# A two-block transformer kernel whose instruction order is drawn up against another model of the machine

## The chip, the cores and the metric

The kernel runs on one core of one Trainium2 chip. The metric is device time in microseconds (us), lower is better; the time of a kernel is the median of its runs. Apart from those runs one execution was recorded by the hardware profiler, and every row in this document is from such a recording.

## The reference, cut to what matters

One sequence of 512 tokens, model width 1024, float32, goes through two blocks. The first block is a block-sparse attention beside a multi-scale pooling, then a squared-ReLU MLP. The second has an RWKV-7 mixer (a recurrence over the tokens), a three-branch sparse attention (NSA), a gated merge of the two, cross-attention to 256 memory tokens, and a convolutional feed-forward net.

```python
def first_block(x, ...):
    proj = rms_norm(x, norm_mix) @ w_in
    q, k, v, u = split(proj)
    a = moba_attention(q, k, v)                 # 8 heads, ALiBi
    p = multiscale_pool(u, w_pool, pool_scale)
    x = x + concat([a, p]) @ w_out
    h = rms_norm(x, norm_mlp)
    x = x + square(relu(h @ w_up)) @ w_down     # 1024 -> 4096 -> 1024
    return rms_norm(x, norm_final)

def second_block(x, mem, ...):
    z = rms_norm(x, norm_mix_2) @ w_in_2
    y_r = rwkv7_mixer(z_r, ...)                 # state = state*w + sa*b + v*k, token by token
    y_n = nsa_mixer(z_q, z_kc, ..., gates)      # 16 heads, 4 kv groups
    gm = sigmoid(z_m)
    merged = gm[0] * (y_r @ w_branch_rwkv) + gm[1] * (y_n @ w_branch_nsa)
    h = x + merged @ w_mix_out
    h = h + cross_attn(rms_norm(h), rms_norm(mem), ...)     # 4 heads
    return h + conv_ffn(rms_norm(h), ffn_up, ffn_conv, ffn_down)   # width 2816
```

## The kernel before

**Products.** Activations lie transposed, 128 features by 512 tokens to a tile. Every large product runs in three passes: both factors are split into a high part in the PE's fast 32-bit format and the remainder, and high x high, high x low and low x high are added up in PSUM. `gemm_g` does this: for each tile of 128 outputs and each group of eight 128-row slices, SP loads a 128x1024 weight tile `ws` (L209), ACT casts it to `wh` (L222), DVE subtracts to get `wl` (L223), and PE runs 24 matmuls of 512 columns (L243 to L245). `ws`, `wh` and `wl` have two buffers each; then `evac`, a function of the caller, takes the result out of PSUM. `gemm_tok_g` (L271 to L273) is the same with the roles of weights and activations exchanged. Products that belong to different streams are told apart by the tag of their PSUM bank: `psg`, `psg_p`, `psg_m`, `psg_b`.

**Stages.** By the trace's time: the first block's projections and attention (about 0 to 200 us), its MLP (to 580), the projections of the second block together with the preparation of the RWKV recurrence (to about 1050), the recurrence, the sparse attention and the merge (to about 1460), and the tail of output product, cross-attention and feed-forward net (to the end). Within a stage generators in Python are interleaved by `weave`: each generator yields an estimate of the PE time of what it has just emitted, and the one that is furthest behind its rate goes on. What comes out is one long program; the two stages in which three kinds of work are mixed are emitted by these two lines:

```python
g.weave(("", g.rwkv_fronts(xs), 245), ("_p", others(), 170))
...
g.weave(("", until("", g.nsa()), 190), ("_b", right(), 240), ("_m", until("_m", g.merge_gates(xs, range(49, 59))), 65))
```

`rwkv_fronts` makes decay, keys and values per pair of heads; in it `head_stats` squares the keys, adds them up on PE (L561), takes the reciprocal root by ten or so small DVE operations (L149 to L155), spreads it with one ACT copy (L570) and turns it back with four PE transposes (L573). `rwkv_solve` inverts small triangular matrices by 31 pairs of DVE operations (L777, L778), each of which needs the pair before. `rwkv_chain` is the recurrence: for each of 8 head pairs and 8 chunks it goes PE (L874), DVE (L875), PE (L888), DVE (L889), PE (L891), DVE (L897), each step needing the one before; `rwkv_finish` ends a head pair with transposes (L919). `nsa_groups` and `attend` are the attention (L311 to L333). `merge_gates` is a plain product, ten tiles of 24 matmuls in the second of the two stages (`psg_m`), and serves to fill PE.

**Order.** The engines run side by side, each through one list of instructions in a fixed order, and wait for each other by semaphores. The lists are not the order in which the Python code emitted the instructions. When the `TileContext` at L1602 closes, the framework plays the program on a model of the machine: whenever an engine is free in the model, it gets the instruction that is ready there and that stands earliest in the program; buffers of a pool are handed out in the same play. The order in which the model started the instructions becomes the list of each engine. The SP and POOL queues, which issue the DMAs, are ordered in the same way. An instruction that the model thought ready early, and that is late on the chip, holds up all that stands behind it on its engine.

## Time and profile before

| | |
|---|---|
| time of the kernel, median of 3 runs | 2091.92 us (2091.23 to 2095.46) |
| the profiled execution | 2094.42 us, its span 2092.6 us |
| busy in that span | PE 2015.6 us, PE weight loads 1635.5, DVE 1308.9, ACT 926.1, POOL 95.4 |
| mean granted clock of the PE | 0.975 |
| HBM | 205.12 MB read, 45.53 MB written, 120 GB/s over the span |

The span runs from the first to the last instruction; the 1.8 us between it and the execution's time lie outside. Busy time of the PE counts matmuls from issue to modelled end, and they overlap, so that a busy PE may still be a PE that does not run at full rate. The granted clock is a mean over the stretch, as a share of full speed (2.4 GHz); the clock has two levels here, 1.2 and 2.4 GHz.

### The profile page before, as it was taken

How to read it: one execution, taken by the hardware profiler on the slowest of the kernel's cores; microseconds unless marked ns; L12 is line 12 of the kernel's file. 1: busy time of each engine (PE TensorE's matmuls, PEld its weight loads, DVE VectorE, ACT ScalarE, POOL GpSimd, SP SyncE). 2: the span in 40 equal slices, each digit the busy share in tenths (PEclk: the TensorE clock that was granted, in tenths of full speed). 3: DMA queues.
4: the chain of work that ended last, by engine and by line, in shares of the span. 5: the costliest groups of instructions: out<-in, count | busy, mean ns of one | idle time of the engine just before them, and what ended most of it. 6: DMA issues, size and time to landing. Idle time of an engine off the chain costs nothing. (4 is left out here: it accounts for less than half of the span.)

```text
span 2092.6 us, 27828 instructions
## 1 busy us (share of the span) xinstructions
PE 2015.6 (96%) x9927; PEld 1635.5 (78%) x9927; DVE 1308.9 (63%) x3007; ACT 926.1 (44%) x1778; POOL 95.4 (5%) x167
## 2 busy tenths in 40 slices
PE   8999999999999999899989899999999999999999
PEld 7778888888887778777767688877878878888887
DVE  5785432554464569777668788878466756666522
ACT  5864531442253233233357477767143443333311
POOL 0000000000003201000120111000000000000000
PEclk9999999999999999999989799999999999999999
DMA  4223333333365655555574454445542123323332
GB/s 161 80 89 95 94 92 100 107 115 117 125 199 159 165 158 164 154 149 175 161 178 109 116 131 129 110 131 160 158 145 81 51 80 91 97 95 92 100 108 83
DMA packets 178266, 256.75 MB, mean 123 GB/s; under 512 B 95408, under 2 KB 109952, under 8 KB 178128
## 3 DMA queue, kind: packets, MB, share of 16 engines
q1 hardware_dynamic: 162832, 231.31, 38.1%
q0 software_dynamic: 15296, 23.66, 4.0%
q8 instruction: 79, 1.29, 0.3%
q14 instruction: 59, 0.48, 0.1%
HBM read 205.12 MB, written 45.53 MB: 120 GB/s over the span
## 5 line engine op out<-in xcount | busy, mean ns | idle before, releaser
L222 ACT CAST wh<-ws 128x1024 fp32r<-128x1024 f32 (+2 forms) x283 | 291.7, 1031 | 699.6 <-PE psg L244 459.4
L223 DVE TENSOR_TENSOR wl<-ws,wh 128x1024 fp32r<-128x1024 f32 (+2 forms) x283 | 339.5, 1201 | 263.5 <-ACT wh L222 262.3
L243 PE MATMUL psg<-xh,wh 128*128 128x512 f32 x984 | 392.1, 399 | 2.9 <-ACT wh L222 2.9
L245 PE MATMUL psg<-xh,wl 128*128 128x512 f32 x984 | 393.6, 400 | 0.0
L244 PE MATMUL psg<-act,wh 128*128 128x512 f32 x912 | 359.7, 395 | 1.1 <-DVE act L166 1.1
L243 PEld LDWEIGHTS psg<-xh,wh 128*128 128x128 f32 x984 | 185.9, 189 | 45.0 <-ACT wh L222 3.7
L245 PEld LDWEIGHTS psg<-xh,wl 128*128 128x128 f32 x984 | 186.1, 189 | 41.6 <-issue 1.2
L244 PEld LDWEIGHTS psg<-act,wh 128*128 128x128 f32 x912 | 171.1, 188 | 42.8 <-DVE act L166 1.5
L243 PE MATMUL psg<-act,wh 128*128 128x512 f32 x496 | 196.2, 397 | 2.8 <-ACT act L165 1.4
L245 PE MATMUL psg<-act,wl 128*128 128x512 f32 x496 | 196.0, 396 | 0.5 <-DVE wl L223 0.5
L244 PE MATMUL psg<-xl,wh 128*128 128x512 f32 x352 | 139.7, 397 | 0.0
L243 PEld LDWEIGHTS psg<-act,wh 128*128 128x128 f32 x496 | 92.8, 187 | 27.3 <-ACT act L165 2.2
L245 PEld LDWEIGHTS psg<-act,wl 128*128 128x128 f32 x496 | 93.0, 187 | 23.8 <-DVE wl L223 1.3
L315 ACT ACTIVATE p<-p,sm 128x128 f32<-128x128 f32 (+3 forms) x160 | 89.6, 561 | 18.8 <-DVE sm L313 17.7
L244 PE MATMUL psg<-x,wh 128*128 128x512 f32 x216 | 88.7, 411 | 0.0
L331 DVE TENSOR_TENSOR pt<-psb,pt 128x512 fp32r<-128x512 f32 (+3 forms) x160 | 75.6, 487 | 18.7 <-ACT pt L330 16.6
L313 DVE CUSTOM_DVE_ANT_0 p<-psa,bias 128x128 f32<-128x128 f32 (+3 forms) x160 | 76.0, 484 | 11.9 <-PE psa L312 9.7
L328 PE MATMUL psb<-ident,p 128*128 128x128 f32 x400 | 79.1, 292 | 2.2 <-DVE p L323 1.2
L330 ACT CAST pt<-psb 128x512 fp32r<-128x512 f32 (+3 forms) x160 | 65.9, 424 | 32.0 <-PE psb L328 29.4
L244 PEld LDWEIGHTS psg<-xl,wh 128*128 128x128 f32 x352 | 66.3, 188 | 14.1
L243 PE MATMUL psg_p<-xh,wh 128*128 128x512 f32 x176 | 72.8, 414 | 0.8 <-ACT f L957 0.6
L244 PE MATMUL psg_p<-x,wh 128*128 128x512 f32 x176 | 72.3, 411 | 0.0
(491 smaller groups left out, 3916.4 us busy)
## 6 DMA issues: line engine op xcount, KB each, us to landing
ws<-in_w_in SPq DMA_DIRECT2D x49, 512.0 KB, 4.0
ws<-in_w_fup SPq DMA_DIRECT2D x44, 512.0 KB, 3.5
ws<-in_w_up SPq DMA_DIRECT2D x32, 512.0 KB, 3.5
ws<-in_w_down SPq DMA_DIRECT2D x32, 512.0 KB, 3.6
ws<-in_w_fdn SPq DMA_DIRECT2D x16, 512.0 KB, 3.6
ws<-in_w_qku SPq DMA_DIRECT2D x12, 512.0 KB, 3.6
ws<-in_w_in POOLq DMA_DIRECT2D x10, 512.0 KB, 4.8
ws<-in_w_out SPq DMA_DIRECT2D x8, 512.0 KB, 3.5
```

Of the source, the lines that this page charges most:

```text
L222: nc.scalar.copy(wh[:, :n], ws[:, :n])
L223: nc.vector.tensor_tensor(wl[:, :n], ws[:, :n], wh[:, :n].bitcast(F32), OP.subtract)
L243: nc.tensor.matmul(p[:, :n], wh[:, s], h[:, :n], start=c + k == 0, stop=False)
L244: nc.tensor.matmul(p[:, :n], wh[:, s], l[:, :n], start=False, stop=False)
L245: nc.tensor.matmul(p[:, :n], wl[:, s], h[:, :n], start=False, stop=last)
L313: nc.vector.tensor_tensor_reduce(pt, ps[:, :w], bias[:, 512 - w:], 1.0, 3e38, OP.add, OP.min, m[:, i:i + 1])
L315: nc.scalar.activation(pt, pt, AF.Exp, bias=m[:, i:i + 1], scale=-1.0, accum_out=s[:, i:i + 1])
L328: nc.tensor.transpose(ps[:, (i - j) * 128:(i - j + 1) * 128], P[i][:, j * 128:j * 128 + 128], self.ident)
L330: nc.scalar.copy(ph[:, :w], ps[:, :w])
L331: nc.vector.tensor_tensor(pl[:, :w], ps[:, :w], ph[:, :w].bitcast(F32), OP.subtract)
```

## The change

One argument is added where the kernel opens the framework's context. The lists of all engines are then drawn up by playing the program on the framework's timeline model instead of on its default one. The rule by which an instruction is picked, the program that is played, every instruction and its operands' shapes, the pools and their numbers of buffers are the same; what can differ is the order on each engine, DMA queues included, which of a pool's buffers a tile gets, and with these the semaphore waits.

```diff
@@ -1599,7 +1599,7 @@
     nc = bacc.Bacc("TRN2", target_bir_lowering=False, num_devices=1)
     A = {k: nc.dram_tensor("in_" + k, v.shape, F32, kind="ExternalInput").ap() for k, v in arrays.items()}
     out = nc.dram_tensor("out_0", (D, T), F32, kind="ExternalOutput").ap()
-    with tile.TileContext(nc) as tc:
+    with tile.TileContext(nc, schedule_with_timeline_sim=True) as tc:
         emit(tc, A, out)
     r = run_bass_kernel_spmd(nc, [{"in_" + k: v for k, v in arrays.items()}], core_ids=[0])
     return np.ascontiguousarray(r.results[0]["out_0"].T)[None]
```

## Rows read from the trace of the kernel before

**Rows 1.** The page: span, and busy time of each engine.

```profile
span 2092.6 us, 27828 instructions
PE 2015.6 (96%) x9927; PEld 1635.5 (78%) x9927; DVE 1308.9 (63%) x3007; ACT 926.1 (44%) x1778; POOL 95.4 (5%) x167
```

**Rows 2.** Busy time by stage: stretch, its length, busy us of each engine, clock, DMA.

```profile
0.00:40.00 40.00, 33.89 (x232) 31.44 (x233) 23.19 (x48) 21.58 (x34) 0.20 (x4) 1.00 0.52 177
40.00:580.00 540.00, 537.50 (x2511) 435.44 (x2509) 285.80 (x516) 242.23 (x407) 0.95 (x1) 1.00 0.33 102
580.00:760.00 180.00, 172.81 (x906) 140.79 (x906) 99.92 (x197) 69.68 (x111) 30.61 (x51) 0.98 0.63 173
760.00:1060.00 300.00, 278.63 (x1419) 225.09 (x1418) 225.25 (x621) 104.17 (x158) 30.49 (x59) 0.96 0.58 163
1060.00:1440.00 380.00, 349.74 (x1999) 287.81 (x1998) 304.32 (x1035) 257.42 (x727) 33.12 (x52) 0.90 0.50 131
1440.00:1720.00 280.00, 274.63 (x1274) 217.47 (x1273) 178.26 (x348) 117.15 (x209) 0.00 (x0) 1.00 0.34 106
1720.00:2080.00 360.00, 359.90 (x1560) 290.93 (x1559) 191.10 (x244) 113.84 (x136) 0.00 (x0) 1.00 0.32 98
2080.00:2092.60 12.60, 8.52 (x37) 6.53 (x35) 1.05 (x2) 0.00 (x0) 0.00 (x0) 1.00 0.05 21
```

**Rows 3.** Waits of PE: total us, times, longest.

```profile
PE psn L573 <- ACT cx L570: 7.6, 1, 7.6
...
PE psn L919 <- ACT y L915: 5.4, 3, 3.0
PE psb_b L874 <- ACT vs L842: 4.9, 1, 4.9
PE psg L243 <- ACT wh L222: 3.7, 3, 2.9
PE psn L561 <- DVE vc L1098: 3.4, 1, 3.4
```

**Rows 4.** PE in order of time around the longest wait: start, duration, instruction.

```profile
870.07 0.40 PE L243 MATMUL psg_p<-xh,wh 128*128 128x512 f32 x1
878.07 1.12 PE L573 MATMUL psn<-ident,cx 128*128 128x128 f32 x4 [7.60 <-ACT cx L570]
878.83 0.78 PE L244 MATMUL psg_p<-x,wh 128*128 128x512 f32 x1
879.41 0.63 PE L245 MATMUL psg_p<-xh,wl 128*128 128x512 f32 x1
...
883.24 0.39 PE L243 MATMUL psg<-xh,wh 128*128 128x512 f32 x1
883.47 0.39 PE L244 MATMUL psg<-x,wh 128*128 128x512 f32 x1
```

**Rows 5.** DVE in order of time over the same stretch.

```profile
869.97 0.16 DVE L566 TENSOR_SCALAR sm<-psn 128x8 f32<-128x8 f32 x1
...
870.98 1.22 DVE L223 TENSOR_TENSOR wl<-ws,wh 128x1024 fp32r<-128x1024 f32 x1
...
876.96 0.16 DVE L155 SCALAR_TENSOR_TENSOR col<-sm,col 128x8 f32<-128x8 f32 x1
```

**Rows 6.** The recurrence's first matmul, by line: x count, ns min/median/max, first and last start.

```profile
L874 PE MATMUL psb_b<-vs,ws x128: 270/275/553, 1068.5 to 1417.3; 128*128 128x128 f32 x128
```

**Rows 7.** Groups by line, 1060 to 1440: count, busy us, mean ns, idle before.

```profile
L897 DVE SCALAR_TENSOR_TENSOR vs<-vs,decay,psb_b 64x64 f32<-64x64 f32 x96 | 26.7, 279 | 8.0 <-PE psb_b L891 5.8
...
L223 DVE TENSOR_TENSOR wl<-ws,wh 128x1024 fp32r<-128x1024 f32 x10 | 12.2, 1220 | 0.1
```

**Rows 8.** The matmuls of `psg_m` alone, three stretches of 20 us; clock next.

```profile
1160.00:1180.00 20.00, 0.00 (x0) 0.00 (x0) 0.00 (x0) 0.87 0.51 146
1180.00:1200.00 20.00, 0.46 (x2) 0.38 (x2) 0.00 (x0) 0.53 0.39 102
1200.00:1220.00 20.00, 7.91 (x27) 4.58 (x26) 0.58 (x1) 1.00 0.46 123
```

## The prediction

> **What bounds the kernel now.** I read the page first, for the share of each engine, then busy time by stage, then the waits of PE, the longest of them in order of time, and last the stage in which the recurrence runs. In the page the reader sees PE busy for all but 77.0 us of its 2092.6 us span and no other engine near that [rows 1]. By stage this falls apart into two kernels [rows 2]. From 40 to 580 us and from 1720 to 2080 us PE is without a gap to speak of (2.5 and 0.1 us idle) at full clock: in the latter 1560 matmuls take 360 us, one every 0.231 us, and an order of instructions can win nothing there, since the same matmuls have to pass. The first 40 us (6.1 us idle) wait for the first inputs, and the last 12.6 us (4.1 us) for the last result to leave. What is left between 580 and 1440 us is 860 us in which three kinds of work are mixed: idle 7.2, 21.4 and 30.3 us, 58.9 together, and a granted clock of 0.98, 0.96 and 0.90, which is 3.6, 12.0 and 38.0 us of full-speed time that PE was not given, 53.6 together. From 1440 to 1720 us another 5.4 us are idle. So this is where a change of order is won or lost: some 860 us out of 2093, with 58.9 us of gaps.
>
> **What such a gap is.** The longest one shows the kind. PE waits 7.6 us in one piece for a copy by ACT [rows 3]. In order of time [rows 4]: at 870.07 us PE runs a matmul of a large product (`psg_p`), then its list has the four transposes of `head_stats` (L573), whose input is late, and they start at 878.07 us. The next in the list is the second pass of that same product, over the weights `wh` of which the first pass had just run: it was ready all the time and stood behind. After the gap the matmuls come 0.58 us apart first, and 0.23 us apart again at 883 us. DVE was what made the input late: the reciprocal root begins at 869.97 us (L566) and its last small operation starts at 876.96 us, because between its links DVE's list has steps of the triangular solve and splits of weights, one of 1.22 us [rows 5]. Both lists were drawn up by a play in which the root was done sooner than it was. This is what another model of the machine can change, and it is the only thing.
>
> **The change part by part.** It removes and adds no instruction and no byte: 9927 matmuls, 3007 DVE and 1778 ACT instructions stay [rows 1], so the sum of work is 0 us on either side, and it is hidden by nothing because it does not change. What moves are places in the lists.
>
> (1) The unmixed stages, 900 us with their two long stretches: 0 us, bounded by their idle time, 2.6 us, on the side of a gain. On the side of a loss the cover is that a weight tile is loaded and split while the eight slices before it run, 24 matmuls of 0.231 us or 5.5 us, against 1.2 us on DVE for a split and about as much on ACT. Only an order that puts several long DVE operations ahead of a split uncovers it; DVE is busy 191 of 360 us there [rows 2], so I take 0.
>
> (2) The gaps of the mixed stages. Nothing in this trace shows the new order, so its worth is bounded by rows: below by nothing (each gap is only traded for another), above by all 58.9 us. Between these I take the five single waits of 2.9 us or more [rows 3]: 7.6 (L573), 4.9 (L874), 3.4 (L561), 3.0 (the longest of the three at L919) and 2.9 (L243), together 21.8 us. A model that has DVE's and ACT's small operations about right will not put a matmul before an input that is 3 us or more away while others are ready; that is the error of the present lists which the rows show. The other 37.1 us are gaps of under 2 us, smaller than the differences between any two orders, and I let them stand as moved.
>
> (3) The clock. Its 53.6 us are bounded the same way, between 0 and all. I take 0: the low clock is deepest where PE's work is thin, and part of it lies under the gaps counted already.
>
> (4) DMA queues and buffers. SP and POOL get a new order too. SP issues a weight load when a buffer comes free; the loads stand under the cover of (1). I take 0 here, and leave a loss to the rivals.
>
> The sum: span 2092.6 - 21.8 = 2070.8 us; with the 1.8 us outside the span 2072.6 us against the profiled execution's 2094.4; and as the median of the runs stands 2.5 us below the profiled execution, 2070 us.
>
> A rule of the Trainium skill speaks for less. "Perfetto Trace Analysis", section "Identifying the Most-Contended Engine", says that matmul busy time is not a good measure of how near PE is to its limit, and that the busy share of weight loads is one. By it the ceiling is lower: weight loads are busy 290.93 of 360 us (80.8%) where PE is full and 653.69 of 860 us (76.0%) in the mixed stages, so that these could shrink to 809 us, by 51 us instead of 112.5 for gaps and clock; the same share of that (21.8 of 58.9) would be 19 us and the time 2073 us. I keep the rows of single waits, which name their places.
>
> **The rivals.**
>
> *The recurrence is served later (slower).* From 1068.5 to 1417.3 us L874 runs for 64 steps [rows 6], two matmuls each: 348.8 us over 63 intervals, 5.54 us a step, in which DVE must be reached three times, for operations of about 0.28 us [rows 7]. DVE is busy 304.3 of 380 us there, with 1035 instructions, 0.294 us on average [rows 2]. If the new lists hand DVE and PE more of the attention's and the product's work as soon as it is ready, each visit of the recurrence finds one more instruction ahead: 3 x 0.294 x 63 = 56 us if the recurrence alone sets the stage. The attention runs beside it to the stage's end, so I count half, 28 us: 2120 us. It decides the sign once a step gets 0.35 us longer (21.8 / 63). For it: DVE has little slack there, and one split in front costs 1.22 us [rows 7]. Against it: the recurrence keeps its place in the program, and the rule of picking is the same.
>
> *The filler is spent early (slower).* The stage's plain product (`psg_m`) fills PE. Where it has none or two matmuls, the granted clock is 0.87 and 0.53; in the next 20 us, with 27, it is 1.00 [rows 8]. A play that finds PE free more often runs this product as soon as its weights are there, and leaves the end of the stage thin. If 100 us more run at 0.70 in place of 0.90, that is 20 us, and 2112 us. The low level is 1.2 of 2.4 GHz, so a matmul there takes twice as long. The Trainium skill points the same way: "Perfetto Trace Analysis", section "Matmul Optimizations", says that PE scales its power with its use and that matmuls should come back to back in batches; the rows just named agree, with 0.53 and 1.00.
>
> *No change.* The new lists differ, but gaps are traded one for one; or the option leaves the lists as they are. 2092 us. For it: two thirds of the time is indifferent to order. Against it: 860 us of three-way mixing rarely come out the same to 4 us.
>
> *More than the five.* All gaps of the mixed stages go: 2092 - 59 = 2033 us. For it: DVE would still have room (629.5 of 860 us busy). Against it: 30.3 of the 58.9 us lie where chains of small steps feed each other.
>
> **How the numbers follow.** The forecast (5 to 35 us faster) gets 0.38, more than that 0.11, no change 0.13, the recurrence served later 0.22, the filler spent early 0.16. What a measurement of this kernel can tell from no change is 0.2%, 4 us. So faster 0.49, same 0.13, slower 0.38. The likeliest case gives 2070 us, with a range of its own of 2057 to 2087. Over all cases I take 2034 (all gaps gone) to 2124 (the first rival and 4 us more); below lie about 0.04, above about 0.12.
>
> **What would show it.** Right: from 580 to 1440 us the same work takes about 840 us, with some 37 us idle, and among PE's waits no single one over 3 us between 600 and 1440 us; L573 is no longer ahead of a product's matmuls for microseconds; the stretches before 580 and after 1440 us are as long as before, to 3 us. The recurrence served later shows as more than 5.9 us from one step of L874 to the next. The filler spent early shows as an end of `psg_m` well before 1400 us and a clock under 0.85 behind it. It would make the prediction wrong if the unmixed stages got gaps: then weight loads or splits are late, and (1) was the step that failed; or if the gaps stayed and others came, then the present model's error was not what made them.

## The result and the profile after

The kernel got slower: 2223.05 us median (2218.63 to 2223.74, 4 runs) against 2093.69 us (2091.23 to 2096.67, 4 runs, one more than ahead of the prediction), a ratio of 1.0625 with a 95% interval of 1.0602 to 1.0648. The forecast was 2070 us, in a range that ended at 2124 us. Both the number and the sign were wrong.

The page of the changed kernel, span and busy time of each engine:

```profile
span 2221.8 us, 27961 instructions
PE 2057.5 (93%) x9927; PEld 1677.9 (76%) x9927; DVE 1322.8 (60%) x3007; ACT 927.5 (42%) x1778; POOL 99.7 (4%) x167
```

The reader sees the same counts as in [rows 1], so no work was added. The span grew by 129.2 us, of which 87.3 us are idle time of PE (164.3 in place of 77.0) and 41.9 us are busy time of the same 9927 matmuls. Most of this is the clock, whose mean over the span fell from 0.975 to 0.952: at its low level (1.2 GHz) PE was busy for 172.6 us in place of 94.9. Matmuls of one shape, first at the low and then at the full level:

```profile
804.41 0.63 PE L243 MATMUL psg<-xh,wh 128*128 128x512 f32 x1
804.84 0.63 PE L244 MATMUL psg<-x,wh 128*128 128x512 f32 x1
...
806.40 0.40 PE L243 MATMUL psg<-xh,wh 128*128 128x512 f32 x1
806.63 0.39 PE L244 MATMUL psg<-x,wh 128*128 128x512 f32 x1
```

They start 0.43 us and 0.23 us apart, so a matmul does not take twice as long at the low level, as the prediction had it, but somewhat less. By these numbers the low level accounts for some 36 of the 41.9 us (an estimate, 77.7 x (1 - 0.23/0.43)).

To see where, both kernels are cut at the same work and not at the same times: at the first L504 (end of the MLP), the first L833 (start of the recurrence stage), the last L333 (end of the sparse attention) and the last L1376 (end of the cross-attention). The busy time by stretch of the kernel before, cut so; columns as in [rows 2]:

```profile
0.00:567.70 567.70, 559.39 (x2648) 455.97 (x2649) 300.51 (x538) 257.03 (x432) 0.20 (x4) 1.00 0.34 106
567.70:1051.90 484.20, 457.35 (x2383) 372.04 (x2382) 328.52 (x837) 176.78 (x271) 57.96 (x104) 0.97 0.59 165
1051.90:1459.40 407.50, 375.23 (x2138) 307.75 (x2136) 326.58 (x1092) 278.89 (x778) 37.22 (x59) 0.91 0.50 131
1459.40:1681.60 222.20, 217.55 (x1014) 173.10 (x1013) 138.63 (x268) 83.07 (x142) 0.00 (x0) 1.00 0.35 107
1681.60:2092.60 411.00, 406.11 (x1752) 326.64 (x1750) 214.65 (x273) 130.31 (x158) 0.00 (x0) 1.00 0.31 95
```

And of the changed kernel:

```profile
0.00:584.80 584.80, 566.43 (x2670) 464.82 (x2671) 301.08 (x539) 257.19 (x432) 0.20 (x4) 0.99 0.33 104
584.80:1088.70 503.90, 461.41 (x2361) 375.80 (x2359) 335.54 (x835) 176.13 (x268) 58.34 (x98) 0.94 0.57 157
1088.70:1592.80 504.10, 431.85 (x2276) 359.95 (x2276) 346.26 (x1107) 287.53 (x787) 41.16 (x65) 0.86 0.44 118
1592.80:1808.60 215.80, 191.45 (x875) 151.00 (x874) 125.42 (x254) 76.50 (x134) 0.00 (x0) 0.98 0.28 86
1808.60:2221.80 413.20, 406.33 (x1752) 326.38 (x1750) 214.54 (x273) 130.18 (x158) 0.00 (x0) 1.00 0.31 95
```

The five differences are +17.1, +19.7, +96.6, -6.4 and +2.2 us. The fourth hides a loss: 139 fewer matmuls fall into it (they ran ahead, into the third), and in it the cross-attention itself, from its first L1356 to its last L1376, went from 68.2 to 85.4 us. So every stretch in which a chain of dependent steps runs beside a plain product lost, and the last one, plain products alone, hardly did.

The waits of PE in the changed kernel, as in [rows 3]:

```profile
PE psg L243 <- ACT wh L222: 11.7, 7, 8.3
PE psn_p L573 <- ACT cx L570: 9.8, 2, 9.2
PE psa L311 <- DVE sm L313: 8.9, 16, 1.7
PE psb_b L888 <- DVE rh L875: 7.8, 19, 0.7
...
PE psg_m L243 <- ACT f L957: 6.4, 2, 5.2
```

The wait on which the forecast rested, at L573, is still there and has grown from 7.6 to 9.2 us. The recurrence, as in [rows 6]:

```profile
L874 PE MATMUL psb_b<-vs,ws x128: 270/275/552, 1116.2 to 1515.8; 128*128 128x128 f32 x128
```

That is 399.6 us over 63 steps, 6.34 us a step in place of 5.54. But the 50.8 us are not spread over the steps: the first eight take 94.6 us in place of 49.2, and the other 55 take 5.54 us each in place of 5.44. Of the third stretch's 96.6 us some 11 lie ahead of the first L874 and some 35 behind the last, where the attention takes 76.9 us to its end in place of 42.1. And the filler, as in [rows 8]; the number before the last two of each row is the clock:

```profile
1180.00:1200.00 20.00, 11.88 (x44) 7.36 (x43) 1.19 (x2) 1.00 0.47 141
1200.00:1220.00 20.00, 3.42 (x14) 2.16 (x12) 0.60 (x1) 0.74 0.64 204
1220.00:1240.00 20.00, 0.00 (x0) 0.00 (x0) 0.00 (x0) 1.00 0.63 163
```

Its last matmul starts at 1203.4 us, ahead of the seventh of 64 steps of the recurrence; before, it lasted to 1425.0 us, past the last step. From 1240 to 1540 us the clock of the 20 us stretches is between 0.60 and 0.91.

Last, what happens to a step of the recurrence while the filler runs. DVE in order of time:

```profile
1197.64 0.30 DVE L889 COPY_PREDICATED vu<-blk,psb_b 128x128 f32<-128x128 int32 x1
1202.73 0.57 DVE L897 SCALAR_TENSOR_TENSOR vs<-vs,decay,psb_b 64x64 f32<-64x64 f32 x2 [4.79 <-PE psb_b L891]
```

PE over the same stretch:

```profile
1197.78 0.50 PE L245 MATMUL psg_m<-xh,wl 128*128 128x512 f32 x1
1198.11 0.39 PE L243 MATMUL psg_m<-xh,wh 128*128 128x512 f32 x1
...
1202.07 0.40 PE L245 MATMUL psg_m<-xh,wl 128*128 128x512 f32 x1
1202.31 0.38 PE L891 MATMUL psb_b<-vu,wl 128*128 128x128 f32 x2
```

DVE has finished L889 at 1197.94 us. The matmul that needs it, L891, starts at 1202.31 us: 18 matmuls of the filler stand between, run without a gap, and DVE is idle for 4.79 us. Since PE has no gap here, no view of PE's waits shows it.

One such place proves little: the kernel before has one of 5.03 us from L889 to L891, with 29 others between. What changed is the mean while the filler runs. Over the first eight steps, from L875 to L888 it is 3.4 us with 13.8 other matmuls between (before: 1.4 us, 6.0), and from L889 to L891 2.3 us with 9.8 (before: 0.9 us, 4.6). Over the later steps the two are nearly as before, 0.46 and 0.90 us in place of 0.48 and 0.80. In the attention it lasts through the stage: from the end of ACT's copy (L330) to the start of the matmul that uses it (L332), each copy taken with its own matmul, 128 times from the first L874 on, the mean is 0.39 us with 1.6 other matmuls between in the kernel before, and 2.01 us with 9.3 in the changed one. (The expectations below give 8.0 for the latter, which counts only to the next L332, also that of another copy.) Ready work waits for its turn, not for its input.

### The profile page after: what moved, and what is told of

It reads as the page before. It is cut to its first block, busy times and chain, and to the rows that moved or that the text cites. A ratio compares the mean times of both kernels' runs of the same rounds, so it can differ in the third digit from the quotient of the medians.

```text
span 2221.8 us, 27961 instructions
## 1 busy us (share of the span) xinstructions
PE 2057.5 (93%) x9927; PEld 1677.9 (76%) x9927; DVE 1322.8 (60%) x3007; ACT 927.5 (42%) x1778; POOL 99.7 (4%) x167
## 4 chain that ended last, share of the span: by engine, by line
PE 37%; DVE 6%; DMA 3%; ACT 3%; issue 2%; SPq 0%; POOL 0%; DVEq 0%; ACTq 0%
PE psg L243 7%; PE psg L244 7%; PE psg L245 7%; PE psg_b L245 1%; PE psg_b L243 1%; PE psg_b L244 1%; PE psb L328 1%; DMA ld<-vd 1%; PE pso L332 1%; PE pso L333 1%; PE psb_b L888 1%; DVE wl L223 1%; ACT p L315 1%; DVE pt L331 1%; DMA yc<-ydr 1%
## 5 line engine op out<-in xcount | busy, mean ns | idle before, releaser
L243 PE MATMUL psg<-xh,wh 128*128 128x512 f32 x984 | 393.5, 400 | 18.7 <-ACT wh L222 10.4
L243 PEld LDWEIGHTS psg<-xh,wh 128*128 128x128 f32 x984 | 186.7, 190 | 64.1 <-ACT wh L222 11.2
L243 PE MATMUL psg<-act,wh 128*128 128x512 f32 x496 | 197.0, 400 | 8.0 <-ACT act L162 3.4
L243 PEld LDWEIGHTS psg<-act,wh 128*128 128x128 f32 x496 | 92.8, 188 | 33.9 <-ACT act L162 4.6
L330 ACT CAST pt<-psb 128x512 fp32r<-128x512 f32 (+3 forms) x160 | 65.0, 423 | 45.4 <-PE psb L328 41.8
L243 PE MATMUL psg_p<-xh,wh 128*128 128x512 f32 x176 | 74.9, 425 | 4.3 <-DVE f L1035 2.6
L245 PE MATMUL psg_p<-xh,wl 128*128 128x512 f32 x176 | 73.4, 417 | 0.0
```

What stands on the lines that cost most here:

```text
L243: nc.tensor.matmul(p[:, :n], wh[:, s], h[:, :n], start=c + k == 0, stop=False)
L245: nc.tensor.matmul(p[:, :n], wl[:, s], h[:, :n], start=False, stop=last)
L330: nc.scalar.copy(ph[:, :w], ps[:, :w])
```

## The experiments

Three theories were tried, in this order. **F**: the independent products stand ahead of the chains on PE. Against F stands **O**: the order of the small operations on DVE and ACT and of the DMA issues is what costs. **P, D, Q**: the list of one engine carries the loss (PE; DVE and ACT; the DMA queues). **L**: the timeline model deals instructions out too early, so that what becomes ready later stands behind them. Against L stands **T**: the times that the model gives to the operations make the difference. Ratios are to the kernel before on the same chip; medians from different chips, on which the kernel before took 2082 to 2094 us, are compared by their ratios only. Each kernel is one layout of the program.

| kernel | ratio (95% interval) | median, us |
|---|---|---|
| changed kernel | 1.0625 (1.0602 to 1.0648) | 2223.05 |
| tl_hold_m | 1.071 (1.0646 to 1.0773) | 2235.86 |
| df_early_m | 1.0121 (1.0068 to 1.0175) | 2111.81 |
| tl_hold_all | 1.1454 (1.1401 to 1.1506) | 2389.79 |
| df_hold_all | 1.1319 (1.1269 to 1.1369) | 2363.33 |
| pin_pe | 1.0529 (1.0508 to 1.0549) | 2191.59 |
| pin_dve | 1.1124 (1.1088 to 1.1161) | 2316.42 |
| pin_act | 1.0963 (1.0927 to 1.0999) | 2283.72 |
| pin_queues | 1.108 (1.1055 to 1.1105) | 2304.92 |
| ahead_pe4 | 1.0114 (1.009 to 1.0138) | 2111.25 |
| ahead_pe16 | 1.0354 (1.0326 to 1.0383) | 2162.71 |
| ahead_pe70 | 1.0971 (1.0942 to 1.0999) | 2293.47 |
| ahead_all2 | 1.0024 (1.0008 to 1.004) | 2092.85 |
| ahead_rest2 | 1.0535 (1.05 to 1.0569) | 2197.7 |
| pin_pe_all2 | 1.0408 (1.0365 to 1.0451) | 2178.06 |
| all2_chain_p185 | 0.9953 (0.9934 to 0.9972) | 2079.76 |
| df_chain_p185 | 1.0104 (1.0088 to 1.0121) | 2109.39 |

### The filler, held back or spent early

tl_hold_m adds one pin to the changed kernel, in `gemm_g`; `keep_in_program_order` is a call of the framework:

```diff
-                    nc.tensor.matmul(p[:, :n], wh[:, s], h[:, :n], start=c + k == 0, stop=False)
+                    m = nc.tensor.matmul(p[:, :n], wh[:, s], h[:, :n], start=c + k == 0, stop=False)
+                    k == 0 and self.sx == "_m" and self.tc.keep_in_program_order(m)
```

> The timeline model as in the changed kernel, but the first matmul of each tile of the filler product psg_m is pinned behind the matmul that stands before it in the program, so that the filler is spread over the recurrence again. Theory F (independent products stand ahead of the dependent chains on PE, and the chains then run bare): the first eight steps of the recurrence take about 50 us again in place of 94.7, and the rest of the stage gets its filler back, so the time falls by 45 to 80 us, to 2143 to 2178 us. Theory O (the order of the small operations on DVE and ACT and of the DMA issues is what costs): the time stays within 15 us of 2223 us.

df_early_m changes a rate in the kernel before:

```diff
-("_m", until("_m", g.merge_gates(xs, range(49, 59))), 65))
+("_m", until("_m", g.merge_gates(xs, range(49, 59))), 400))
```

> The default model as in the kernel before, but the filler product is emitted at a rate of 400 in place of 65, so that all 240 of its matmuls stand ahead of step 17 of the recurrence, as in the changed kernel. Theory F: 40 to 75 us slower than before, 2132 to 2167 us, with PE idle for about 15% of the stage after the filler. Theory O: within 15 us of 2092 us, since every other stream is emitted as before.

The filler spent early costs 1.2%, some 25 us, in the default model's lists: less than F's 40 to 75, and more than O's 15. Held back in the timeline model's lists it gives nothing back, as O had it. The recurrence of tl_hold_m:

```profile
L874 PE MATMUL psb_b<-vs,ws x128: 270/294/583, 1109.6 to 1522.0; 128*128 128x128 f32 x128
```

And of df_early_m:

```profile
L874 PE MATMUL psb_b<-vs,ws x128: 270/275/551, 1072.5 to 1436.3; 128*128 128x128 f32 x128
```

That is 412.4 us (6.55 a step) with the filler spread, to 1581.5 us, and 363.8 us (5.77 a step) with the filler spent before step 11. The first eight steps take 74.3 and 76.5 us, the other 55 6.14 and 5.22 us each. So under either model an early filler lengthens the first steps and shortens the later ones, and under the timeline model both are longer than under the default one with the filler alike. L330 to L332 goes with the model: 1.81 us with the pin and 0.36 us in df_early_m.

### All products held in the order of the program

The same pin without the condition on the stream, and one on the first matmul of each weight tile in `gemm_tok_g`, with either model.

> The timeline model, with the first matmul of each weight tile of every large product pinned behind the matmul before it in the program, in all stages. Theory F: nearly all of the loss comes back, 2080 to 2130 us, the first block's attention and the cross-attention each 15 us or so shorter than in the changed kernel. Theory O: 2180 us or more.

> The same pins with the default model. Theory F: the default model's lists have the products near their place in the program already, so 2070 to 2115 us, and within 25 us of the same pins with the timeline model. Theory O: as the kernel before, and 80 us or more faster than the pins with the timeline model.

Both are far slower, and 1.3% apart, where F had both near the kernel before and O had the second there. F is out as a remedy: products that may not slide at all cost more than products that slide too far. That the two come near each other says only that a stiff order drowns the difference of the models.

### One engine bound to the default model's list

The program is laid out twice in one build, and each instruction of one engine gets an order edge to its predecessor in the first layout:

```diff
+    with tile.TileContext(n0) as t0:
+        emit(t0, A0, o0)
     with tile.TileContext(nc, schedule_with_timeline_sim=True) as tc:
         emit(tc, A, out)
+        pin(tc, n0, ['PE'], old)
...
+            if e in last:
+                tc.add_manual_dep(here[i.name], last[e], info, reason="pin")
+            last[e] = i.name
```

> The program is laid out twice: first with the default model, whose list of PE is read off, then with the timeline model, in which the matmuls are bound to that list; the lists of DVE, ACT, SP and POOL are the timeline model's, drawn up around it. Theory P (the loss sits in the list of PE: products stand ahead of the chains' matmuls, and the matmuls of the recurrence stand behind more of the attention's): 2085 to 2125 us. Theory D (it sits in the lists of DVE and ACT, whose small operations of one chain stand behind those of another): 2180 us or more. Theory Q (it sits in the DMA queues): 2180 us or more.

> As pin_pe, but DVE alone is bound to the default model's list. Theory D: 2090 to 2150 us. Theories P and Q: 2190 us or more. If the lists lose only together, because each fits the others' times, every one of the four bound lists gives a part back, 20 to 60 us each.

> As pin_pe, but ACT alone is bound to the default model's list. Theory D: DVE gives more back than ACT, since it is busier; here 2150 to 2200 us. Theories P and Q: 2190 us or more.

> As pin_pe, but the two DMA queues, SP and POOL, are bound to the default model's lists. Theory Q (weights and keys are fetched late, because the timeline model takes a transfer for longer or shorter than it is): 2100 to 2150 us. Theories P and D: 2200 us or more.

Each theory fails on its own kernel: PE's list gives back 1.0% of the time before, some 20 us, and each of the others loses a further 3.4 to 5.0%, 70 to 105 us. Nor does every bound list give a part back, as lists that lose only together were to. No engine's list carries the loss by itself, or else binding costs something of its own. pin_pe_all2, further down, decides between these.

### How far ahead the play deals

In the framework's code the timeline model has a setting for each engine of how many instructions it may have accepted and not yet finished, 35 for PE and 12 for the others. The section on the change and the prediction had taken the rule of dealing for the same under both models. The edit, for PE and 4:

```diff
+    deep = TRN2Spec.ENG_ISSUE_QUEUE_DEPTH
+    TRN2Spec.ENG_ISSUE_QUEUE_DEPTH = {**deep, mybir.EngineType.PE: 4}
     with tile.TileContext(nc, schedule_with_timeline_sim=True) as tc:
         emit(tc, A, out)
+    TRN2Spec.ENG_ISSUE_QUEUE_DEPTH = deep
```

It alters how the lists are drawn up (and, with them, which buffer a tile gets) and nothing of the program, of the model's operation times or of the chip.

> The timeline model lets an engine accept instructions before it executes them, and its setting for PE is 35; the play deals an instruction out when it is accepted. Here the setting is 4 for PE and unchanged for the others; it is put back once the lists are drawn up, and nothing else differs from the changed kernel. Theory L (looking ahead: a matmul that becomes ready finds up to 35 others already dealt in front of it, so the lists place it late): most of the loss comes back, 2085 to 2130 us, and from the end of ACT's copy (L330) to the matmul that uses it (L332) fewer than 3 other matmuls stand, where the changed kernel has 8.0 on average and the kernel before 1.6. Theory T (the times that the model gives to the operations make the difference): within 20 us of 2223 us.

> As ahead_pe4 with the setting 16 for PE. Theory L: between the two, 2140 to 2190 us. Theory T: within 20 us of 2223 us.

> As ahead_pe4 with the setting 70 for PE, twice that of the changed kernel. Theory L: slower still, 2235 to 2290 us. Theory T: within 20 us of 2223 us.

> As ahead_pe4 with the setting 2 for all engines (35 for PE and 12 for the others in the changed kernel). Theory L: the loss is gone, 2060 to 2095 us, so no slower than the kernel before, and what is left against it is what the operation times of this model are worth, which the prediction had put at 22 us. Theory T: within 20 us of 2223 us.

The time follows the setting: 1.0114, 1.0354, 1.0625 (the changed kernel, 35) and 1.0971 for 4, 16, 35 and 70. With 2 on all engines 1.0024 is left. T, by which all four were to be at 2223 us, is out. Cut as above, every stretch that lost in the changed kernel grows with PE's setting from 4 to 70 (us; the last column is the mean from L330 to L332):

| kernel | to the end of the MLP | to the recurrence stage | to the end of the attention | cross-attention | L330 to L332 |
|---|---|---|---|---|---|
| before | 567.7 | 484.2 | 407.5 | 68.2 | 0.39 |
| ahead_all2 | 565.0 | 472.1 | 424.3 | 72.7 | 1.01 |
| ahead_pe4 | 567.0 | 470.2 | 434.2 | 72.8 | 0.95 |
| ahead_pe16 | 576.4 | 474.5 | 476.4 | 80.3 | 1.62 |
| changed, 35 | 584.8 | 503.9 | 504.1 | 85.4 | 2.01 |
| ahead_pe70 | 592.3 | 542.4 | 516.0 | 91.2 | 2.07 |

Three numbers of L missed by a little: ahead_pe70 is 3.5 us above its range, ahead_all2 is 0.24% slower than the kernel before where it was to be no slower, and from L330 to L332 there stand 4.6 other matmuls at 4, not fewer than 3. This handover is no measure of the loss by itself: it has nearly stopped growing at 35, and it is 1.01 us in ahead_all2, which lost next to nothing. The page of ahead_all2:

```profile
span 2091.2 us, 27942 instructions
PE 2002.3 (96%) x9927; PEld 1640.9 (78%) x9927; DVE 1314.5 (63%) x3007; ACT 922.3 (44%) x1778; POOL 99.2 (5%) x167
```

The page of ahead_pe70:

```profile
span 2293.4 us, 27940 instructions
PE 2086.9 (91%) x9927; PEld 1701.0 (74%) x9927; DVE 1319.8 (58%) x3007; ACT 928.3 (40%) x1778; POOL 95.2 (4%) x167
```

The longest waits of PE in ahead_all2:

```profile
PE psb_b L888 <- DVE rh L875: 8.9, 4, 6.0
PE psb_b L874 <- DVE vs L897: 5.4, 8, 2.3
PE psb L1138 <- DVE f L1135: 4.9, 1, 4.9
PE psa_b L879 <- ACT yi L858: 4.7, 1, 4.7
```

The long wait at L573 is gone (1.5 us in 5 pieces are left at it, none over 0.4), as the prediction had said of a model with better times. Others of 4.7 to 6.0 us have come, and idle time is 88.9 us (2091.2 - 2002.3) in place of 77.0. The table tells where: 12.1 us were won in the second stretch, and 16.8 lost in the third, in which PE's idle time rose from 32.3 to 50.4 us.

### Which engines' settings, and what binding costs

ahead_rest2 has `{e: n if e == mybir.EngineType.PE else 2 for e, n in deep.items()}`; pin_pe_all2 is pin_pe with `{e: 2 for e in deep}`.

> The timeline model with its setting of 35 for PE, and 2 in place of 12 for ACT, DVE, SP and POOL. Theory L in its narrow form (PE's looking ahead carries the loss): at most 30 us come back, 2190 to 2225 us. Theory L in its wide form (every engine's looking ahead counts alike): half or more comes back, under 2160 us.

> PE bound to the default model's list as in pin_pe, and the other lists drawn up by the timeline model with the setting 2 on all engines, which without a binding took 1.0024 of the time before. If the other engines' looking ahead is what keeps pin_pe slow, this is level with the kernel before too, 2080 to 2110 us. If a list from another play costs by itself, because the rest of the play is then fitted around an order that it would not have chosen, it stays at 2140 to 2195 us, and the four bound kernels say nothing of one engine's share.

L holds in its narrow form, with PE's setting as the main part: the other engines' settings are worth 0.9% (1.0625 to 1.0535), PE's alone 5.1% (1.0625 to 1.0114 at 4). And a binding costs by itself: with 2 on all engines the free play is at 1.0024, and with PE bound to a list that ran the kernel before in 2092.72 us it is at 1.0408. So it seems that the lists of one play fit each other, and the four bound kernels say nothing of one engine's share.

### The operation times, with the looking ahead gone

Two edits of the program, under either model: the recurrence's instructions count as 400 places earlier in the program, and the product beside the fronts has another rate.

```diff
+    def prio(self, gen, k):
+        while True:
+            with self.tc.high_priority(k):
+                w = next(gen, self)
+            if w is self:
+                return
+            yield w
...
-self.side_by_side([self.rwkv_chain(pr, out, *ops), operands(), last])
+self.side_by_side([self.prio(self.rwkv_chain(pr, out, *ops), 400), operands(), last])
...
-g.weave(("", g.rwkv_fronts(xs), 245), ("_p", others(), 170))
+g.weave(("", g.rwkv_fronts(xs), 245), ("_p", others(), 185))
```

> As ahead_all2 (setting 2 on all engines), with two edits of the program: the recurrence's instructions get a priority 400 places further ahead, and the product beside the fronts is emitted at a rate of 185 in place of 170. If the operation times of the timeline model are worth something once nothing is dealt out too early, this is the version that shows it: 2055 to 2080 us, faster than before. If they are worth nothing, it stays within 10 us of 2090 us.

> The same two edits of the program with the default model. If a gain of all2_chain_p185 comes from the edits and not from the model, it shows here too, 2055 to 2080 us; if it comes from the model, this stays within 10 us of 2090 us.

The page of all2_chain_p185:

```profile
span 2076.6 us, 27967 instructions
PE 1985.9 (96%) x9927; PEld 1632.5 (79%) x9927; DVE 1312.1 (63%) x3007; ACT 919.5 (44%) x1778; POOL 98.8 (5%) x167
```

It is the fastest version here, 0.9953 of the kernel before, about 10 us: clear of its interval, but small, and of one layout. The same edits make the default model's kernel 1.0% slower, against an expected 2055 to 2080 or within 10 us of 2090. So an edit of the program and the model that draws up the lists can't be judged apart. The 2079.76 us lie on the border between the two cases that the expectation had told apart, so that the worth of the operation times is not settled by it.

## Why the prediction was wrong, point by point

**The step that failed** stands in front of all the sums: that the model of the machine changes when an input is thought to be ready, "and it is the only thing", and, against the first rival, that "the rule of picking is the same". It is not. The changed play deals an instruction when an engine of the model accepts it, and the model's PE accepts up to 35 ahead. A chain's matmul whose input gets ready meanwhile stands behind all of them on the list, and the list is what the chip runs. Changing that one number moves the time from 1.0971 over 1.0625 to 1.0114. With 2 on all engines 1.0024 is left, so the looking ahead carries the loss: that is shown. That ready matmuls of the chains are passed over longer, in the recurrence's first eight steps and in the attention throughout, is seen in the trace, but how the 129 us divide among such places was not measured, since binding the list of one engine costs by itself.

**(1) The unmixed stages, 0 us.** Right for 1808.6 us to the end (+2.2 us) and for the MLP (367.7 us from 200 us on before, 369.8 from 215 us on). Wrong for the first block and the cross-attention, 17.1 and 17.2 us. The prediction called 40 to 580 us a stretch without a gap and meant that order can do nothing there. In the first block, when the 113th of the attention's 208 matmuls (L311 to L333) starts, 127 matmuls of the product beside it have started since 50 us in the kernel before, and 229 in the changed one; the rest of the attention then runs with little beside it. A stretch that is full was safe here only where it held no chain.

**(2) The five waits, -21.8 us.** Failed in the changed kernel: L573 has 9.2 us, and a wait of 8.3 us at L243 is new. With the looking ahead taken down to 2 four of the five waits do go (L573, L874 and L243 have none over 0.5 us left for the same input, and L561 waits 3.1 us for another one; L919 keeps 3.2 us), but idle time does not fall. "Each gap is only traded for another", the lower bound of this step, is what happened: ahead_all2 is at 1.0024. The worth of the other operation times by themselves came out as nothing in sum (12 us won before the recurrence, 17 lost in its stage), and not as 21.8 us.

**(3) The clock, 0.** Failed: 41.9 us of the 129.2 are busy time, 30.5 of them from the recurrence stage and the stretch behind it together, where the clock went from 0.91 to 0.86 and from 1.00 to 0.98. The prediction held that part of the low clock lies under gaps already counted and took nothing for it. The clock fell where PE had less to do: from 1100 to 1120 us PE was busy for 10.6 us and had 0.66, from 1140 to 1200 us it was busy for 58.6 of 60 us and had 1.00. The Trainium skill ("Perfetto Trace Analysis", section "Matmul Optimizations") says that PE scales its power with its use; these stretches agree. The early filler does not decide it: behind the filler the clock is 0.84 in the changed kernel (1236.1 to 1504.9 us) but 0.91 in df_early_m (1175.9 to 1425.1), and it is 0.86 in tl_hold_m, whose filler still runs (1210.1 to 1510.0), against 0.91 in the kernel before (1137.4 to 1406.1). It goes with the model.

**(4) Queues and buffers, 0.** Not settled. pin_queues was to test it, and binding costs by itself.

**The rivals.** The marks of both slower ones came: 6.34 us a step against the 5.9 that was to show the first, and a filler that ended at 1203 us against "well before 1400", with a clock of 0.84 behind it. The second came as described. The first came only on average and by another mechanism: it was to be one more instruction on DVE at each of three visits, 0.9 us a step, but steps 9 to 64 took 5.54 us, under its mark, and the eight before lost 45.4 us, some 28 of them at the two handovers to PE counted above, with up to 75 other matmuls between, 41 of them filler (19.9 us from L875 to L888 in the first step). So the two were not separate, and they were priced singly, at 28 and 20 us, and in one stage; the setting for PE moves them together with the first block and the cross-attention. Priced together they are 48 us, and the recurrence stage alone lost 96.6. Spent early, the filler costs 25 us when nothing else changes (df_early_m), near the 20 it was given. What neither rival had is the attention: it was to cover half of a slower recurrence, and it slowed itself (L330 to L332) and ended some 35 us later behind the last step than before.

**What would have warned.** The diff names a model, and the prediction asked only what that model knows of durations. When the play deals belongs to the model too, and the trace of the kernel before does not show it; a range that ended at one rival's price had no room for it.

## What to carry to other kernels

A list scheduler is a model and a rule of dealing, and here better times in the model would not have helped, since it fixed the order earlier: ask first how far ahead of execution each choice is made. Idle time shows inputs that are late, but not ready work behind ready work; for a chain beside a plain product, measure from the end of one link to the start of the next, and count what stands between, as means over a stage and beside the same count of the kernel before. The rates and priorities tried here did not carry over from one scheduler to the other, nor did single lists: swap one part only together with a new fit.

## What was not expected of the chip

Busy time of PE is not a property of the work. The same 9927 matmuls were busy for 1985.9 us in all2_chain_p185 and for 2086.9 us in ahead_pe70, 101 us or 5% apart by order alone, with mean granted clocks of 0.978 and 0.934. At the low level PE was busy for 79.1 and 233.5 us of it; by the 0.43 and 0.23 us above some 72 of the 101 us are the clock's (an estimate), and what the rest is stays open.
